# One more pair by block products, and sums of down weights moved: a SwiGLU, token mixer, SwiGLU layer on one core

## The chip, the core and the metric

The kernel runs on one core of a Trainium2 chip. The core has TensorE (PE in the profile, PEld for its weight loads), VectorE (DVE), ScalarE (ACT), GpSimd (POOL) and SyncE (SP), which here only issues DMAs. The metric is the device time of one launch in microseconds, the median of several runs. Before the change: 1127.27 us, median of 3 runs (1127.23 to 1127.75).

## What is computed

One decoder layer on x of 512 tokens by 1024, all in float32. The change touches its first part alone, a half-step SwiGLU block:

```python
def swiglu(x, w_gate, w_up, w_down):
    return (jax.nn.silu(x @ w_gate) * (x @ w_up)) @ w_down

h = rms_norm(x, ffn1_pre[l])
x = x + 0.5 * rms_norm(swiglu(h, ffn1_w_gate[l], ffn1_w_up[l], ffn1_w_down[l]), ffn1_post[l])
...
x = x + rms_norm(y, mix_post[l])
h = rms_norm(x, ffn2_pre[l])
x = x + 0.5 * rms_norm(swiglu(h, ffn2_w_gate[l], ffn2_w_up[l], ffn2_w_down[l]), ffn2_post[l])
```

The hidden width D_FF is 2816, 22 blocks of 128. The token mixer in the middle (y) stays as it is.

## The kernel before

**Precision.** Each float32 operand is split in two reduced parts: `split` (L110) casts the high part on ScalarE (L112) and subtracts it on VectorE (L119) for the low part. `mm3` (L139) then makes three matmuls of one: high by high, high by low, low by high. Names `whi` and `wlo` are the two parts of a weight tile, `xh_t` and `xl_t` those of the tokens.

**Gate and up.** The function `ffn` walks over 11 pairs of hidden blocks (256 columns of each weight). A pair has two forms.

- As single units (`classical`): four units, gate and up of each block, each 8 contraction tiles x 3 matmuls with all 512 tokens as 512 columns, 96 matmuls. Each unit needs its own 128x1024 piece of weights, split just before. The very first four units run as two halves of 256 tokens, since the tokens arrive in blocks of 128.
- By block products (`strassen`): gate and up of the pair are cut in blocks of contraction half and token half, and seven products of 24 matmuls with 256 columns replace the eight; 168 matmuls. The weights come as two tiles of the tag `raw` (three places), the first with the upper contraction half of gate (a11) and up (a21), the second with the lower half, up first (a22), then gate (a12). VectorE forms s1 = a21 + a22 (L377), a21 = a11 - a21 (L379), s2 = s1 - a11 (L383) and s2 = a12 - s2 (L388); each weight block is then split in high and low part. The products run in the order a11, a21, s2, a12, s1, a22, s2, and the second needs the difference a21. The other factor is sums of tokens in four kinds (`token_sums`, L507), made once per part.

The range `STRASSEN` (L48) says which pairs take the second form: in the first part pairs 3 to 10.

**Tokens' sums.** In the second part the blocks of tokens are kept whole when they are transposed (`full`, L226, copies from PSUM). In the first part they are not: `join` (L531) adds the high and low parts again, eight times, before the sums. The steps are handed out after single units by `STEPS` (L52), three each behind blocks 2 to 5.

**Sums of down weights.** The down projection of the part is also done by block products. It needs sums of the blocks of each pair's down weights. They are formed ahead, while gate and up run: the four blocks b11, b12, b21, b22 of a pair are loaded, `down_sums` (L481) overwrites them with four differences on VectorE (L484), and they are stored to a DRAM tensor `tdram` (L338, L494), to be read again by the down products. `weight_sums(p)` does this within pair p; pairs 10 and 9 are done ahead, in pairs 0 and 1 (`AHEAD`). `SUM_TAGS` names the buffers of each pair (KB, x, V, of: 128x512 each; other pairs use a `raw` tile).

**Down.** `ffn_down` (L579) runs seven products over the pairs: B11, T2, T3, T1, B21, B22, T4. For the last one, the first `EARLY` = 5 weights (T4 of pairs 0 to 4) are loaded during the product B21 into the place of `xl` and split before it begins.

**Order.** Each engine runs its list in order and waits on semaphores. The lists are made by a scheduler that reorders the program's instructions within their dependences; `issue_after` holds an instruction behind another. SP's list issues all large DMAs, in order; a DMA that waits for a buffer holds back those behind it. Buffers are places of a tag, taken in turn.

Of the kernel before, what the change touches and what calls it, by code (L numbers as in the profile page):

```python
# [12 lines left out]
F32 = mybir.dt.float32  # L13
# [14 lines left out]
NF = DFF // P  # L28
# [16 lines left out]
SPLIT_TAGS = dict(X=["Q"] * 4 + ["KA"] * 2, O=["V"] * 2 + ["KA"] * 2 + ["KB"] * 4 + ["SP"] * 11 + ["PT"] * 3,  # L45
                  Y=["PT"] * 5 + ["W"] * 2 + ["CB"] + ["Q"] * 4)
T_TAGS = ["NN"] * 3 + ["N"] + ["PT"] * 8 + ["CB"]
STRASSEN = range(3, NF // 2), range(1, NF // 2)  # L48
AHEAD = {0: 10, 1: 9}
SUM_TAGS = {2: ["KB"] * 4, 3: ["x"] * 4, 4: ["x"] * 4, 5: ["V"] * 4, 6: ["x"] * 4, 7: ["V"] * 4,  # L50
            8: ["of"] * 2 + ["V"] * 2}
STEPS = (0, 3, 3, 3, 3), (4, 2)  # L52
EARLY = 5
HOLD_TAGS = ["W"] * 2 + ["Q"] * 4 + ["KA"] * 2 + ["V"] * 2 + ["CB", "ring"]
PS_BUFS = dict(S=3, T=2, V=1, F=2)
# [4 lines left out]
OPEN = ("SS", "TT", "SS", "FF")  # L60
# [3 lines left out]
class Layer:  # L64
# [237 lines left out]
    def ffn(self, n, wg, wu, wd, post, finish, xsrc, tags, nps, aside=None):  # L302
# [5 lines left out]
        nc = self.nc  # L308
# [20 lines left out]
        def weight_sums(p):  # L329
            if n or p in AHEAD.values():  # L330
                return
            if p in SUM_TAGS:
                self.early_sums(p, wd, [self.slot(tag) for tag in SUM_TAGS[p]])
                return
            r = self.raw(wd[2 * p * P:(2 * p + 2) * P].rearrange("(e p) d -> p e d", p=P), [2, D])
            with self.tc.issue_after(self.last_rest):
                self.down_sums(*[r[:, e, h * S:(h + 1) * S] for e in range(2) for h in range(2)])
            nc.sync.dma_start(self.tdram[p], r.rearrange("p e (h d) -> p (e h) d", h=2))  # L338

        def block(src):  # L340
# [10 lines left out]
        def strassen(p):  # L351
# [95 lines left out]
        for p in range(NF // 2):  # L447
# [28 lines left out]
                self.split(hi, lo, ev)  # L476
            X.append(x)
            E.append((hi, lo))
        self.ffn_down(E, X, Y, wd, post, finish, xsrc)

    def down_sums(self, b11, b12, b21, b22):  # L481

        for out, x, y in ((b11, b12, b11), (b12, b22, b12), (b22, b22, b11), (b21, b21, b22)):
            self.nc.vector.tensor_sub(out, x, y)  # L484

    def early_sums(self, p, wd, places):

        blocks = [(i, h) for i in range(2) for h in range(2)]
        for (i, h), v in zip(blocks, places):
            self.nc.sync.dma_start(v, wd[(2 * p + i) * P:(2 * p + i + 1) * P, h * S:(h + 1) * S])  # L490
        with self.tc.issue_after(self.last_rest):
            self.down_sums(*places)
        for (i, h), v in zip(blocks, places):
            self.nc.sync.dma_start(self.tdram[p][:, 2 * i + h], v)  # L494

# [11 lines left out]
    def token_sums(self):  # L507


        nc = self.nc  # L510
        H = S // 2
        places = []
        for tag in T_TAGS:
            v = self.slot(tag, F32R, (P, D if tag == "NN" else S))
            places += [v[:, o:o + S] for o in range(0, v.shape[1], S)]
        kept, self.whole = self.whole, {}
        self.tsum = [([], []) for _ in range(4)]
        steps = []
        for c in range(2):
            hi, lo = [[v.rearrange("p (k c) -> p k c", k=2) for v in g]  # L520
                      for g in (places[8 * c:8 * c + 4], places[8 * c + 4:8 * c + 8])]
            if kept:
                whole = [kept[h][i][c] for i, h in ((0, 0), (1, 1), (0, 1), (1, 0))]
            else:
                whole = [self.slot("x").rearrange("p (k c) -> p k c", k=2) for _ in range(4)]
            f1, f2, f3, f4 = whole
            for i in range(4):
                for o, v in zip(self.tsum[i], (hi[i], lo[i])):
                    o.extend(v[:, k] for k in range(2))

            def join(dst, i, h, c=c):  # L531
                ks, cs = slice(4 * i + 2 * c, 4 * i + 2 * c + 2), slice(h * H, (h + 1) * H)
                nc.vector.tensor_add(dst, self.xht[:, ks, cs].bitcast(F32), self.xlt[:, ks, cs].bitcast(F32))

            def sub(dst, x, y):
                nc.vector.tensor_sub(dst, x, y)

            def parts(i, hi=hi, lo=lo, whole=whole):
                self.split(hi[i], lo[i], whole[i])

            def s1(f1=f1, f3=f3, join=join):
                join(f3, 0, 1)
                join(f1, 0, 0)
                sub(f1, f3, f1)

            def s2(f1=f1, f2=f2, f3=f3, join=join):
                join(f2, 1, 1)
                sub(f3, f2, f3)
                sub(f2, f2, f1)

            def s3(f2=f2, f4=f4, join=join):
                join(f4, 1, 0)
                sub(f4, f4, f2)

            def d1(f1=f1, f3=f3):
                sub(f1, f3, f1)

            def d2(f1=f1, f2=f2, parts=parts):
                sub(f2, f2, f1)
                parts(1)  # L560

            def d3(f2=f2, f3=f3, parts=parts):
                sub(f3, f2, f3)
                parts(2)

            def d4(f2=f2, f4=f4, parts=parts):
                sub(f4, f4, f2)
                parts(3)

            if kept:  # L570
                steps.append((d1, d3, d2, lambda p=parts: p(0), d4))
            else:
                steps += [s1, s2, lambda p=parts: p(0), s3, lambda p=parts: (p(1), p(2)), lambda p=parts: p(3)]
        if kept:
            a, b = steps
            return [a[0], a[1], b[0], b[1], a[2], b[2], a[3], b[3], a[4], b[4]]
        return steps

    def ffn_down(self, E, X, Y, wd, post, finish, xsrc):  # L579

        nc = self.nc
        NP = NF // 2
# [130 lines left out]
        def between():  # L713
            scaled(2, 0, c[0])
            r = self.rstd([ms[2, 0], ms[2, 1]], 2.0)
            while self.pending:
# [765 lines left out]
    def run(self, out):  # L1482
# [30 lines left out]
        with self.tc.manual_schedule(engines={ET.Activation, ET.DVE, ET.PE}):  # L1513
# [108 lines left out]
```

## Time and profile before

| | |
|---|---|
| median of 3 runs | 1127.27 us |
| the profiled execution, its own time | 1127.8 us |
| its span in the profile | 1125.6 us |
| mean granted clock of TensorE | 0.998 |
| gate and up of the first part, pairs 1 to 10 | from 37.1 to 242.0 us |
| pair 1, pair 2, pair 3 begin on TensorE | 37.1, 58.9, 80.6 us |

A page of the profile gives busy times of each engine over the whole span; views of the trace give the time line of one engine (start, duration, engine, line, operation, out<-in with partitions x elements; in brackets the idle time ahead and what ended it), the waits, and busy times by stretch. In the time line `SPq` rows are issues of DMAs, not their landings. The tile names are the program's with their numbers left out.

### The profile page before, as it was taken

How to read it: one execution, taken by the hardware profiler on the slowest of the kernel's cores; microseconds unless marked ns; L12 is line 12 of the kernel's file. 1: busy time of each engine (PE TensorE's matmuls, PEld its weight loads, DVE VectorE, ACT ScalarE, POOL GpSimd, SP SyncE). 2: the span in 40 equal slices, each digit the busy share in tenths (PEclk: the TensorE clock that was granted, in tenths of full speed). 3: DMA queues.
4: the chain of work that ended last, by engine and by line, in shares of the span. 5: the costliest groups of instructions: out<-in, count | busy, mean ns of one | idle time of the engine just before them, and what ended most of it. 6: DMA issues, size and time to landing. Idle time of an engine off the chain costs nothing.

```text
span 1125.6 us, 18656 instructions
## 1 busy us (share of the span) xinstructions
PE 1115.7 (99%) x6998; PEld 1004.2 (89%) x6998; DVE 911.2 (81%) x1565; ACT 646.8 (57%) x1169; POOL 79.2 (7%) x112
## 2 busy tenths in 40 slices
PE   9999999999999999999999999999999999999997
PEld 8889999998889987778888998888999999998886
DVE  7889999879677889687666688976898888979674
ACT  5435555567564778677565634645555555558562
POOL 1000000000012033243000000001000000000000
PEclk9999999999999999999999999999999999999999
DMA  9986665578863652211477758683323434356862
GB/s 318 331 283 224 185 208 173 153 267 293 265 206 108 196 132 85 68 37 47 147 246 237 243 174 289 203 290 121 101 87 126 129 112 126 100 187 228 290 224 82
DMA packets 153086, 206.04 MB, mean 183 GB/s; under 512 B 19842, under 2 KB 98210, under 8 KB 152740
## 3 DMA queue, kind: packets, MB, share of 16 engines
q1 hardware_dynamic: 152992, 204.85, 56.2%
q8 instruction: 55, 0.90, 0.3%
q14 instruction: 35, 0.29, 0.1%
q10 hardware_dynamic: 4, 0.00, 0.0%
HBM read 165.45 MB, written 39.37 MB: 182 GB/s over the span
## 4 chain that ended last, share of the span: by engine, by line
PE 90%; DVE 5%; ACT 2%; issue 1%; POOL 1%; DMA 1%; POOLq 0%; DVEq 0%; ACTq 0%
PE pb_F L141 11%; PE pb_F L143 11%; PE pb_F L142 11%; PE pb_S L143 8%; PE pb_S L142 8%; PE pb_S L141 8%; PE pb_T L143 6%; PE pb_T L142 6%; PE pb_T L141 6%; PE pb_V L143 3%; PE pb_V L142 3%; PE pb_V L141 3%; PE pb_V L1060 2%; PE pb_T L1045 1%; DVE SP_s L785 1%
## 5 line engine op out<-in xcount | busy, mean ns | idle before, releaser
L112 ACT CAST whi<-raw 128x1024 fp32r<-128x1024 f32 (+1 forms) x213 | 217.7, 1023 | 245.6 <-issue 71.1
L119 DVE TENSOR_TENSOR wlo<-raw,whi 128x1024 fp32r<-128x1024 f32 (+1 forms) x213 | 252.9, 1190 | 91.8 <-ACT whi L112 89.9
L141 PE MATMUL pb_F<-xh_t,whi 128*128 128x512 f32 (+1 forms) x392 | 142.0, 362 | 0.2 <-DVE Q_s L1270 0.2
L142 PE MATMUL pb_F<-xl_t,whi 128*128 128x512 f32 (+1 forms) x392 | 141.1, 360 | 0.0
L143 PE MATMUL pb_F<-xh_t,wlo 128*128 128x512 f32 (+1 forms) x392 | 141.0, 360 | 0.0
L112 ACT CAST whi<-tmp_t 128x1024 fp32r<-128x1024 f32 x55 | 57.6, 1048 | 57.4 <-PE pb_S L142 22.4
L119 DVE TENSOR_TENSOR wlo<-tmp_t,whi 128x1024 fp32r<-128x1024 f32 x55 | 67.3, 1224 | 23.2 <-ACT whi L112 21.8
L141 PEld LDWEIGHTS pb_F<-xh_t,whi 128*128 128x128 f32 x392 | 74.2, 189 | 9.9 <-DVE Q_s L1270 0.4
L143 PEld LDWEIGHTS pb_F<-xh_t,wlo 128*128 128x128 f32 x392 | 74.2, 189 | 9.6
L142 PEld LDWEIGHTS pb_F<-xl_t,whi 128*128 128x128 f32 x392 | 74.3, 190 | 9.3
L141 PE MATMUL pb_S<-xh_t,whi 128*128 128x256 f32 (+1 forms) x232 | 68.4, 295 | 0.0
L143 PE MATMUL pb_S<-xh_t,wlo 128*128 128x256 f32 (+1 forms) x232 | 68.3, 294 | 0.0
L142 PE MATMUL pb_S<-xl_t,whi 128*128 128x256 f32 (+1 forms) x232 | 68.3, 294 | 0.0
L1036 POOL TENSOR_SCALAR SP_s<-SP_s,st_t 128x384 f32<-128x384 f32 (+2 forms) x48 | 47.8, 1010 | 103.8 <-DVE st_t L972 76.3
L163 POOL TENSOR_TENSOR rs_t<-rs_t,mhalf_t 128x1 f32<-128x1 f32 x24 | 17.1, 711 | 538.1 <-DVE rs_t L159 538.0
L142 PE MATMUL pb_T<-xl_t,whi 128*128 128x256 f32 (+1 forms) x184 | 53.9, 293 | 0.0
L143 PE MATMUL pb_T<-xh_t,wlo 128*128 128x256 f32 (+1 forms) x184 | 53.8, 293 | 0.0
L141 PE MATMUL pb_T<-xh_t,whi 128*128 128x256 f32 (+1 forms) x184 | 53.7, 293 | 0.0
L141 PEld LDWEIGHTS pb_S<-xh_t,whi 128*128 128x128 f32 x232 | 44.5, 192 | 1.0
L142 PEld LDWEIGHTS pb_S<-xl_t,whi 128*128 128x128 f32 x232 | 44.5, 192 | 1.0
L143 PEld LDWEIGHTS pb_S<-xh_t,wlo 128*128 128x128 f32 x232 | 44.5, 192 | 0.9
L785 DVE CUSTOM_DVE_ANT_0 SP_s<-pb_S,W_s 128x128 f32<-128x128 f32 (+2 forms) x92 | 37.9, 441 | 7.0 <-PE pb_S L780 4.8
(839 smaller groups left out, 3425.3 us busy)
## 6 DMA issues: line engine op xcount, KB each, us to landing
raw<-in_ffn_w_up_dram SPq DMA_DIRECT2D x38, 512.0 KB, 4.9
raw<-in_ffn_w_gate_dram SPq DMA_DIRECT2D x37, 512.0 KB, 5.0
raw<-in_w_in_dram SPq DMA_DIRECT2D x18, 1024.0 KB, 5.5
raw<-in_ffn_w_down_dram SPq DMA_DIRECT2D x14, 1024.0 KB, 5.8
raw<-tdram SPq DMA_DIRECT2D x14, 1024.0 KB, 6.5
NN_s<-in_ffn_w_down_dram SPq DMA_DIRECT2D x22, 512.0 KB, 5.0
tdram<-NN_s SPq DMA_DIRECT2D x22, 512.0 KB, 4.4
odram<-ring_s SPq DMA_DIRECT2D x36, 128.0 KB, 3.2
```

Of the source, the lines that this page charges most:

```text
L112: self.last_cast = self.nc.scalar.copy(dsthi, src).ins
L119: self.last_rest = self.nc.vector.tensor_sub(dstlo, src, dsthi.bitcast(F32)).ins
L141: mm(out, lhi, rhi, start=start, stop=False, skip_group_check=skip)
L142: mm(out, lhi, rlo, start=False, stop=False, skip_group_check=skip)
L143: mm(out, llo, rhi, start=False, stop=stop, skip_group_check=skip)
L163: nc.gpsimd.tensor_tensor(out=r, in0=v, in1=self.mhalf, op=OP.pow)
L785: nc.vector.tensor_tensor_reduce(p, s, w, -1.0, FLOOR, OP.add, OP.min, st_m)
L1036: nc.gpsimd.tensor_scalar(pp, pp, st[:, 1, t:t + 1], None, op0=OP.mult)
L1045: nc.tensor.transpose(b[:, o + (t - kk) * P:o + (t - kk + 1) * P], pt[pn][:, po + kk * P:po + (kk + 1) * P], self.ident)
L1060: self.nc.tensor.matmul(out[:, kk * P:S], v, pp, start=first and kk == 0 and pi == 0, stop=False, skip_group_check=True)
```

## The change

The pair 2 of the first part takes block products instead of single units. The tokens' sums have to be ready one pair sooner: tokens 256 to 511 are now kept whole (eight copies on ScalarE), tokens 0 to 255 are still joined (four times instead of eight), and the steps are handed out as 5, 3 and 2 behind blocks 1 to 3, the last two inside pair 2. All sums of down weights from pair 2 on move one step later: those of pair p are made within pair p + 1. For the pairs 0, 1, 2, 9 and 10 the fourth difference (b21 - b22, after b22 has become b22 - b11) isn't formed there: b21 is stored as it is, and the last down product loads T2 and b21 of these five pairs and subtracts.

```diff
-STRASSEN = range(3, NF // 2), range(1, NF // 2)
+STRASSEN = range(2, NF // 2), range(1, NF // 2)
 AHEAD = {0: 10, 1: 9}
-SUM_TAGS = {2: ["KB"] * 4, 3: ["x"] * 4, 4: ["x"] * 4, 5: ["V"] * 4, 6: ["x"] * 4, 7: ["V"] * 4,
+DEFER = 0, 1, 2, 9, 10
+SUM_TAGS = {2: ["KB"] * 4, 3: ["x"] * 4, 4: ["V"] * 4, 5: ["x"] * 4, 6: ["V"] * 4, 7: ["of"] * 2 + ["V"] * 2,
             8: ["of"] * 2 + ["V"] * 2}
-STEPS = (0, 3, 3, 3, 3), (4, 2)
+STEPS = (5, 3, 2), (4, 2)
...
             rest_sums()
-            weight_sums(p)
+            if p - 1 in STRASSEN[n]:
+                weight_sums(p - 1)
...
-        for out, x, y in ((b11, b12, b11), (b12, b22, b12), (b22, b22, b11), (b21, b21, b22)):
+        for out, x, y in ((b11, b12, b11), (b12, b22, b12), (b22, b22, b11), (b21, b21, b22))[:3 + last]:
             self.nc.vector.tensor_sub(out, x, y)
...
-            def join(dst, i, h, c=c):
-                ks, cs = slice(4 * i + 2 * c, 4 * i + 2 * c + 2), slice(h * H, (h + 1) * H)
-                nc.vector.tensor_add(dst, self.xht[:, ks, cs].bitcast(F32), self.xlt[:, ks, cs].bitcast(F32))
+            def join(dst, i, c=c):
+                ks = slice(4 * i + 2 * c, 4 * i + 2 * c + 2)
+                nc.vector.tensor_add(dst, self.xht[:, ks, 0:H].bitcast(F32), self.xlt[:, ks, 0:H].bitcast(F32))
...
-        nc.sync.dma_start(xl[:, 0:EARLY].bitcast(F32), weights["T4"](0, EARLY))
+        if defer:
+            for k, o, m in ((0, 0, 3), (3, NP - 2, 2)):
+                for v, nm in ((xl, "T2"), (xh, "T4")):
+                    nc.sync.dma_start(v[:, k:k + m].bitcast(F32), weights[nm](o, m))
+        else:
+            nc.sync.dma_start(xl[:, 0:EARLY].bitcast(F32), weights["T4"](0, EARLY))
...
-            self.split(xh[:, ks], xl[:, ks], xl[:, ks].bitcast(F32))
+            src = xl[:, ks].bitcast(F32)
+            if defer:
+                d4 = self.sbt("tmp", [P, 2, S], bufs=2)[:, 0:ks.stop - k]
+                with self.tc.issue_after(self.last_rest):
+                    nc.vector.tensor_sub(d4, xh[:, ks].bitcast(F32), src)
+                src = d4
+            self.split(xh[:, ks], xl[:, ks], src)
...
-            t2 = self.norm_T(2, g, OPEN[2], sq2)
+            t2 = self.norm_T(2, g, OPEN[2], sq2, whole=True)
...
-            t3 = self.norm_T(3, g, OPEN[3], r=r3)
+            t3 = self.norm_T(3, g, OPEN[3], r=r3, whole=True)
```

The product of the down projection gets a first and a last index for this, since pairs 0, 1, 2, 9 and 10 come first in T4 and the walk then goes over pairs 3 to 8.

Two places show how the lists move. The first is SP's list in pair 1, where the weights of pair 2 are requested. Before: `raw_707` and `raw_738` are the gate and up weights of pair 2, `raw_604` is a tile of pair 1's down weights after its sums, `KB_s` are pair 9's down blocks.

```order
L490 DMA KB_s_681<-in_ffn1_w_down_dram 128x512
L475 DMA odram_73<-W_s_360 128x512
L490 DMA KB_s_682<-in_ffn1_w_down_dram 128x512
L95 DMA raw_707<-in_ffn1_w_gate_dram 128x8x256
L95 DMA raw_738<-in_ffn1_w_up_dram 128x8x256
L338 DMA tdram_72<-raw_604 128x2048
L494 DMA tdram_72<-KB_s_679 128x512
L494 DMA tdram_72<-KB_s_680 128x512
L494 DMA tdram_72<-KB_s_682 128x512
L494 DMA tdram_72<-KB_s_681 128x512
```

After, on SP at the same place: `raw_715` and `raw_718` are the two weight tiles of pair 2 in halves, `raw_622` is pair 1's tile of down sums, `KB_s_690` to `693` are pair 9's blocks, of which `692` is stored without a difference.

```order
L492 DMA KB_s_692<-in_ffn1_w_down_dram 128x512
L492 DMA KB_s_693<-in_ffn1_w_down_dram 128x512
L492 DMA x_s_1888<-in_ffn1_w_down_dram 128x512
L496 DMA tdram_72<-KB_s_692 128x512
L362 DMA raw_715<-in_ffn1_w_gate_dram 128x4x256
L362 DMA raw_715<-in_ffn1_w_up_dram 128x4x256
L339 DMA tdram_72<-raw_622 128x2048
L496 DMA tdram_72<-KB_s_690 128x512
L496 DMA tdram_72<-KB_s_691 128x512
L496 DMA tdram_72<-KB_s_693 128x512
L362 DMA raw_718<-in_ffn1_w_up_dram 128x4x256
L362 DMA raw_718<-in_ffn1_w_gate_dram 128x4x256
```

Pair 2's weights were two requests in a row ahead of pair 1's store; now the second tile stands behind that store and three more, and the first behind the store of pair 9's block as it came.

The second place is VectorE's list where TensorE goes from pair 1 to pair 2. Before, the last splits of pair 2's units and the tokens' steps stand here (`x_s` and `PT_s` are the tokens' sums, `KB_s_779` to `782` pair 2's down blocks):

```order
L484 TENSOR_TENSOR KB_s_779<-KB_s_780,KB_s_779 128x512
L467 TENSOR_TENSOR ring_s_530<-SP_s_695,ring_s_530 128x256
L484 TENSOR_TENSOR KB_s_780<-KB_s_782,KB_s_780 128x512
L468 TENSOR_TENSOR CP_s_506<-W_s_531,ring_s_530 128x256
L119 TENSOR_TENSOR Q_s_701<-ring_s_530,Q_s_700 128x512
L484 TENSOR_TENSOR KB_s_782<-KB_s_782,KB_s_779 128x512
L119 TENSOR_TENSOR wlo_796<-raw_707,whi_795 128x1024
L484 TENSOR_TENSOR KB_s_781<-KB_s_781,KB_s_782 128x512
L119 TENSOR_TENSOR wlo_825<-raw_738,whi_824 128x1024
```

After, on VectorE at the same place: the low part of a11, then s1 (`tmp_t_721`), the difference a21 (in `raw_715`), s2 (`tmp_t_722`), a product of pair 1 (`W_s_550`) and the low part of a21 (`wlo_758`):

```order
L120 TENSOR_TENSOR wlo_729<-raw_715,whi_728 128x1024
L378 TENSOR_TENSOR tmp_t_721<-raw_715,raw_718 128x1024
L380 TENSOR_TENSOR raw_715<-raw_715 128x1024
L384 TENSOR_TENSOR tmp_t_722<-tmp_t_721,raw_715 128x1024
L439 TENSOR_TENSOR W_s_550<-W_s_550,pb_S_661 128x512
L120 TENSOR_TENSOR wlo_758<-raw_715,whi_757 128x1024
L467 TENSOR_TENSOR SP_s_705<-ring_s_549,W_s_550 128x256
L120 TENSOR_TENSOR wlo_787<-tmp_t_722,whi_786 128x1024
```

What stood there waited for one weight tile at a time; now everything from `tmp_t_721` on stands behind the up half of the second tile.

More of the change, by code (lines that the diff above doesn't have):

```diff
@@ L336, in weight_sums @@
             with self.tc.issue_after(self.last_rest):
-                self.down_sums(*[r[:, e, h * S:(h + 1) * S] for e in range(2) for h in range(2)])
+                self.down_sums(*[r[:, e, h * S:(h + 1) * S] for e in range(2) for h in range(2)], p not in DEFER)
             nc.sync.dma_start(self.tdram[p], r.rearrange("p e (h d) -> p (e h) d", h=2))
@@ L478, in ffn, with down_sums @@
             E.append((hi, lo))
-        self.ffn_down(E, X, Y, wd, post, finish, xsrc)
-    def down_sums(self, b11, b12, b21, b22):
-        for out, x, y in ((b11, b12, b11), (b12, b22, b12), (b22, b22, b11), (b21, b21, b22)):
+        self.ffn_down(E, X, Y, wd, post, finish, xsrc, () if n else DEFER)
+    def down_sums(self, b11, b12, b21, b22, last=True):
+        for out, x, y in ((b11, b12, b11), (b12, b22, b12), (b22, b22, b11), (b21, b21, b22))[:3 + last]:
             self.nc.vector.tensor_sub(out, x, y)
@@ L491, in early_sums @@
         with self.tc.issue_after(self.last_rest):
-            self.down_sums(*places)
+            self.down_sums(*places, p not in DEFER)
         for (i, h), v in zip(blocks, places):
@@ L515, in token_sums @@
             places += [v[:, o:o + S] for o in range(0, v.shape[1], S)]
+        joined = 0 not in self.whole
+        if joined:
+            self.new_whole(0)
         kept, self.whole = self.whole, {}
@@ L521, in token_sums @@
                       for g in (places[8 * c:8 * c + 4], places[8 * c + 4:8 * c + 8])]
[L522 to L526, printed above, removed]
+            f1, f2, f3, f4 = whole = [kept[h][i][c] for i, h in ((0, 0), (1, 1), (0, 1), (1, 0))]
             for i in range(4):
@@ L539, in parts, with d1 @@
                 self.split(hi[i], lo[i], whole[i])
[L541 to L555, printed above, removed]
+            def d1(f1=f1, f3=f3, join=join):
+                if joined:
+                    join(f1, 0)
                 sub(f1, f3, f1)
@@ L568, in d4, with ffn_down @@
                 parts(3)
[L570 to L579, printed above, removed]
+            steps.append((d1, d3, d2, lambda p=parts: p(0), d4, lambda f4=f4, join=join: join(f4, 1)))
+        a, b = steps
+        return [a[0], a[1], b[0], b[1], a[2], b[2], a[3], b[3]] + ([a[5], b[5]] if joined else []) + [a[4], b[4]]
+    def ffn_down(self, E, X, Y, wd, post, finish, xsrc, defer):
         nc = self.nc
@@ L605, in split_next, with product @@
             parts[nm].append((hi, lo))
-        def product(a, wname, banks, start, stop, side=None, tail=0, keep=None, between=None, pre=()):
+        def product(a, wname, banks, start, stop, side=None, tail=0, keep=None, between=None, pre=(), begin=0, end=NP):
             held = []
@@ L613, in mm @@
                 hi, lo = a(k, t)
-                self.mm3(banks[t], hi, lo, w[0], w[1], start and k == 0, stop and k == NP - 1, True)
-            for k, w in enumerate(pre):
+                self.mm3(banks[t], hi, lo, w[0], w[1], start and k == 0, stop and k == end - 1, True)
+            for k, w in pre:
                 for t in range(2):
                     mm(t, k, w)
-            for k0 in range(len(pre), NP, 4):
-                n = min(4, NP - k0)
+            for k0 in range(begin, end, 4):
+                n = min(4, end - k0)
                 r = self.raw(weights[wname](k0, n), [n, S])
@@ L623, in product @@
                     m = min(2, n - k1)
-                    if keep and k0 + k1 + m > NP - tail:
+                    if keep and k0 + k1 + m > end - tail:
                         for j in range(m):
@@ L632, in product @@
                         k = k0 + k1 + j
-                        if k >= NP - tail:
+                        if k >= end - tail:
                             held.append((k, (hi[:, j], lo[:, j])))
@@ L720, in ffn_down @@
         product(half(parts["O"], 256), "T4", c, False, True, None, NP - EARLY, list(HOLD_TAGS), between,
-                [(xh[:, k], xl[:, k]) for k in range(EARLY)])
+                [(k, (xh[:, i], xl[:, i])) for i, k in enumerate(defer or range(EARLY))],
+                *((3, NP - 2) if defer else (EARLY, NP)))
         r = self.rstd([self.meansq(c[1], S, 2.0), ms[3, 1]], 2.0)
```

## The prediction

> **What bounds the kernel now.** I read the page first: TensorE is busy for the whole span. Then the list of who waited for whom, for TensorE alone.
>
> ```profile
> PE 1115.7 (99%) x6998; PEld 1004.2 (89%) x6998; DVE 911.2 (81%) x1565; ACT 646.8 (57%) x1169; POOL 79.2 (7%) x112
> PE pb_V L1511 <- POOL ident_t masks.py:199: 1.5, 1, 1.5
> PE pb_S L779 <- DVE SP_s L988: 0.2, 1, 0.2
> ```
>
> After the 1.5 us at the start no wait of TensorE is longer than 0.2 us, and none lies in the first part's gate and up. So the time is a sum of matmul slots. The change can gain only what it takes out of that sum; a wait that it adds counts in full. Freeing VectorE gains nothing by itself, since nobody on TensorE waits for it now.
>
> The stretches of the gate and up tell how near the next bound is. Columns: stretch, its length, then the busy time of TensorE, its weight loads, VectorE, ScalarE and GpSimd, the granted clock, the DMA share, GB/s.
>
> ```profile
> 0.00:37.20 37.20, 35.75 (x246) 32.62 (x247) 26.75 (x44) 20.84 (x37) 4.88 (x14) 1.00 1.00 334
> 12.00:37.20 25.20, 25.20 (x213) 25.15 (x212) 21.34 (x33) 13.83 (x23) 2.80 (x4) 1.00 1.08 369
> 37.20:58.85 21.65, 21.65 (x97) 17.91 (x96) 20.83 (x34) 6.95 (x10) 2.35 (x2) 1.00 0.90 304
> 59.00:80.77 21.77, 21.77 (x99) 18.04 (x98) 16.77 (x25) 6.73 (x10) 0.00 (x0) 1.00 0.89 286
> 100.92:121.07 20.15, 20.15 (x170) 20.15 (x170) 20.03 (x27) 10.92 (x15) 0.00 (x0) 1.00 0.67 215
> ```
>
> Pair 1 is the third row, pair 2 the fourth, pair 4 (by block products) the fifth. There VectorE is full too (20.03 of 20.15 us), and the DMA queue is close to full until pair 3 (0.89 to 1.08 of its 16 engines). Pair 2 is where VectorE had slack (16.77 of 21.77).
>
> **The change, part by part.** *Matmuls.* The time line of TensorE gives the slots; its columns are start, duration, then the instruction.
>
> ```profile
> 58.86 0.39 PE L141 MATMUL pb_S<-xh_t,whi 128*128 128x512 f32 x1
> 59.08 0.39 PE L142 MATMUL pb_S<-xl_t,whi 128*128 128x512 f32 x1
> 80.62 0.28 PE L141 MATMUL pb_S<-xh_t,whi 128*128 128x256 f32 x1
> 100.88 0.28 PE L141 MATMUL pb_T<-xh_t,whi 128*128 128x256 f32 x1
> 101.00 0.28 PE L142 MATMUL pb_T<-xl_t,whi 128*128 128x256 f32 x1
> 121.04 0.28 PE L141 MATMUL pb_S<-xh_t,whi 128*128 128x256 f32 x1
> ```
>
> Pair 2 runs from 58.86 to 80.62: 21.76 us for 96 matmuls of 512 columns (4 units x 8 x 3), 0.2267 each. Pair 4 runs from 100.88 to 121.04: 20.16 us for 168 of 256 columns (7 products x 8 x 3), 0.120 each. The change puts 168 of the second kind for 96 of the first: **-1.60 us**, and no other matmul changes. The Trainium skill, "TensorE: Matmul & The Clock Gate", section "Wait — 56ns, not 53.3ns?", puts the warm distance of matmuls at N / 2.4 GHz + 2.5 ns, so 215.8 and 109.2 ns here; by that the estimate is 20.72 - 18.34 = 2.4 us of gain. The rows show 226.7 and 120, so I take 1.60.
>
> *What pair 2 now needs earlier.* As single units, pair 2 needed one split weight after another. By block products the second product needs a21 = a11 - a21, formed behind s1 = a21 + a22, and a22 comes with the **second** weight tile. Before, this stood in front of pair 3:
>
> ```profile
> 75.22 1.23 DVE L377 TENSOR_TENSOR tmp_t<-raw 128x1024 f32<-128x1024 f32 x1 [2.16 <-DMA raw<-in_ffn_w_up_dram]
> 76.36 0.68 DVE L437 TENSOR_TENSOR ring_s<-ring_s,pb_T 128x512 f32<-128x512 f32 x1
> 79.03 1.22 DVE L379 TENSOR_TENSOR raw<-raw 128x1024 f32<-128x1024 f32 x1
> 80.16 1.22 DVE L383 TENSOR_TENSOR tmp_t<-tmp_t,raw 128x1024 f32<-128x1024 f32 x1
> 81.44 1.23 DVE L119 TENSOR_TENSOR wlo<-raw,whi 128x1024 fp32r<-128x1024 f32 x1
> 82.59 0.68 DVE L437 TENSOR_TENSOR W_s<-W_s,pb_V 128x512 f32<-128x512 f32 x1
> ```
>
> VectorE idled 2.16 us for the load and began s1 at 75.22; the low part of a21 was ready at 81.44 + 1.23 = 82.67, and TensorE wanted it at 80.62 + 24 x 0.120 + 0.24 = 83.74. A margin of 1.07 us, behind a load. In the changed order s1, a21, s2, a product of 128x512 and the low part stand directly behind each other: 3 x 1.14 + 0.60 + 1.22 = 5.24 us from s1's start S (steps of 1.14 and 0.60 from these rows' starts), 5.29 with 0.05 to be noticed. TensorE reaches pair 2 at 58.86 as before and wants that low part at 58.86 + 2.88 + 0.24 = 61.98. So TensorE **waits S - 56.7 us**, and everything turns on when the second tile's up half (a22) lands.
>
> *When it lands.* Up to and with that load the changed SP order holds 18.74 MB (tiles counted from the code). Three readings. (a) If the queue never idles: 334 GB/s x 37.2 us = 12.4 MB by 37.2, the other 6.3 MB at 369 GB/s take 17.1 us: S = 54.3, no wait. (b) Before, 18.74 MB end with the last of four stores to tdram from KB:
>
> ```profile
> L494 SPq DMA_DIRECT2D tdram<-KB_s x1: 320/320/320, 55.3 to 55.3; - x1
> DMA to landing us min/median/max: 4.2/4.2/4.2
> ```
>
> issued at 55.3, landed 4.2 later: S = 59.5, a wait of 2.8. (c) By its chain of waits:
>
> ```profile
> 29.66 0.35 SPq L338 DMA_DIRECT2D tdram<-raw  x1
> ...
> 46.94 0.38 SPq L95 DMA_DIRECT2D raw<-in_ffn_w_up_dram  x1
> 47.54 0.40 SPq L338 DMA_DIRECT2D tdram<-raw  x1
> L338 SPq DMA_DIRECT2D tdram<-raw x1: 402/402/402, 47.5 to 47.5; - x1
> DMA to landing us min/median/max: 8.7/8.7/8.7
> tdram<-KB_s SPq DMA_DIRECT2D x12, 256.0 KB, 4.8
> KB_s<-in_ffn_w_down_dram SPq DMA_DIRECT2D x12, 256.0 KB, 5.7
> raw<-in_ffn_w_up_dram SPq DMA_DIRECT2D x38, 512.0 KB, 4.9
> tdram<-raw SPq DMA_DIRECT2D x2, 1024.0 KB, 8.6
> ```
>
> On SP the loads for pair 2 now stand behind the store of pair 9's unsummed block, which waits for that block's load, which waits for a KB place that a store of pair 10's sums has to leave. Those stores follow the reload of the third raw place, whose old content must have been stored first; that store lands at about 38.2 now (29.66 issue and 8.6), so they go out near 38.4. Then 4.8 (store) and 5.7 (load) give 48.9 for pair 2's first issue. Its first tile and a store of 1 MB are 2.10 MB, the same as the two rows at 46.94 and 47.54, which took 47.54 + 8.7 - 46.94 = 9.3 us: 58.2. Three KB stores and the a22 half, 1.31 MB at 304 to 369 GB/s, take 3.6 to 4.3: S = 62.1, a wait of 5.4. I take the middle of (b) and (c), **S = 60.8 and a wait of 4.1 us**, because both are this queue's own rows, while (a) needs a queue that the rows show idling (0.90 from 37.2 on). The ends stay: 0 to 5.4.
>
> The Trainium skill, "DMA: Bandwidth & Descriptors", section "Anatomy of one DMA — SWDGE (gpsimd) path", fits a DMA as 2.0 us + bytes / 436 GB/s. By it chain (c) is 38.4 + 2.6 + 2.6 + 2.0 + 7.8 = 53.4 (an estimate), and the wait is gone. It is fitted for GpSimd's path, and the row of 512 KB here has 4.9 us where it gives 3.2; so I count it to the first rival.
>
> *VectorE's work.* Pair 2 gets seven low parts for four (3 x 1.14), four sums of 1.14 and two of 0.60: 9.2 us more. Out go the fourth down sums of five pairs and four sums of tokens (9 x 0.60 = 5.4), and one step of delay moves four sums per pair behind. In pair 2: 16.77 - 4 x 0.60 (its down sums go to pair 3) + 9.2 = 23.6, less some five steps of 0.60 on the tokens that now stand ahead of it = 20.6, against 20.16 of TensorE. That is 0.4 over, and VectorE's idle time in front of S, or the wait itself, hides it: nothing, or 0.4 us if that cover is gone. ScalarE gets eight copies of 128x256 between 21 and 25 us:
>
> ```profile
> 29.70 1.05 ACT L112 CAST whi<-raw 128x1024 fp32r<-128x1024 f32 x1 [6.17 <-DMA raw<-in_ffn_w_gate_dram]
> ```
>
> There it idled 6.17 us for a load; nothing.
>
> *The last down product.* Three more subtractions (2.9 us) and 1.31 MB more of loads:
>
> ```profile
> 285.00:315.00 30.00, 30.00 (x134) 24.85 (x133) 20.61 (x24) 16.09 (x19) 0.00 (x0) 1.00 0.78 258
> ```
>
> VectorE has 9.4 us free in these 30, and the sums are wanted only after the product before. Nothing; up to 1 us if the next weight tile, queued behind the added loads, comes late.
>
> *Sum.* -1.6 + 4.1 = **+2.5 us**. The profiled execution took 1127.8 us (span 1125.6 and 2.2 around it), 0.5 over the median of 1127.27; I add to the median: **1129.8**. What a measurement here can tell from no change is about 0.2%, 2.25 us.
>
> **The rivals.** *The load comes in time* (for: reading (a), since the loads before it are issued earlier than they were; against: (b), (c), and the same sum that waited 2.16 us for a load before pair 3). The wait is 0 to 2.8 us, the net -1.6 to +1.2: 1125.7 to 1128.5. This is the other side, not slower; it decides at S = 59.5 and is pure gain from S = 56.7. *The load comes later still*: pauses of the queue as long as the 2.16 us above, or the late weight tile of the down products; net +3.8 to +5.3, up to 1132.6. Against: the queue ahead is full and needs no start. *The wider gain*: 2.4 us by the skill's slot and no wait, 1124.9; the rows of 0.120 speak against it. That the change doesn't do what it says can be ruled out by the order: 72 more matmul rows, as 168 - 96.
>
> **How the numbers follow.** The forecast, a wait of 2.8 to 5.4 us, 1128.5 to 1131.1: 0.58. In time: 0.25. Later: 0.14. Wider gain: 0.03. The bound of 2.25 over cuts the forecast at a wait of 3.9, 0.36 of it above. So slower by over 0.2%: 0.36 + 0.14 = 0.50; within: 0.22 + 0.25 = 0.47; faster: 0.03. The range takes in the pure gain, 1125.7, and the late load, 1132.6; the likeliest case alone has 1128.5 to 1131.1.
>
> **What would show it.** Pair 2 should hold 168 matmuls, and outside one gap last 20.16 us. The gap should stand 24 matmuls into pair 2, with "whi" of ScalarE and then "wlo" of VectorE as releaser; VectorE's s1 should show idle time of several us in front of it, ended by the load of the up weights. If that row starts before 56.7 I am wrong on the queue; if TensorE waits in pair 3 or later, on VectorE; if near 315 to 325, on the last down product.

## The result, and the profile after

The changed kernel takes 1137.30 us, the median of 4 runs (1136.96 to 1138.64), against 1127.51 before (the median of four runs; 1127.27 was that of the first three): a ratio of 1.0085, 95% interval 1.0073 to 1.0097. That is 9.8 us slower, where +2.5 was forecast and 1132.6 was the end of the range. The side was right, the size was not. The profiled execution took 1136.97 us and spans 1134.9, 9.3 more than the span before.

First the busy times on the page of the changed kernel, then from its list of TensorE's waits the three longest besides the 1.5 us at the start, which the kernel before has too (line waited for, us in total, times, longest):

```profile
PE 1117.7 (98%) x7070; PEld 1007.9 (89%) x7070; DVE 916.9 (81%) x1569; ACT 654.4 (58%) x1185; POOL 75.8 (7%) x112
PE pb_V L142 <- ACT whi L113: 5.9, 1, 5.9
PE pb_V L144 <- DVE wlo L120: 0.9, 1, 0.9
PE pb_F L218 <- DVE tmp_t L213: 0.8, 1, 0.8
```

TensorE's time line (start, duration) shows where the two long ones stand:

```profile
61.84 0.28 PE L144 MATMUL pb_T<-xh_t,wlo 128*128 128x256 f32 x1
68.01 0.58 PE L142 MATMUL pb_V<-NN_s,whi 128*128 128x256 f32 x1 [5.89 <-ACT whi L113]
68.39 0.41 PE L143 MATMUL pb_V<-N_s,whi 128*128 128x256 f32 x1
69.74 0.58 PE L144 MATMUL pb_V<-NN_s,wlo 128*128 128x256 f32 x1 [0.94 <-DVE wlo L120]
...
74.30 0.28 PE L142 MATMUL pb_S<-NN_s,whi 128*128 128x256 f32 x1
```

The gap stands after 24 matmuls of pair 2, at its second product, and behind it the matmuls are slow: the 22 from 69.74 to 74.30 take 4.56 us, where 22 x 0.120 = 2.64 is their time at the usual step. That is 1.9 us more. The windows name the reason in the column of the granted clock (third from the end):

```profile
62.00:64.00 2.00, 0.12 (x1) 0.00 (x0) 0.00 (x0) 0.00 (x0) 0.00 (x0) 1.00 1.09 358
66.00:68.00 2.00, 0.00 (x0) 0.00 (x0) 2.00 (x3) 1.04 (x1) 0.00 (x0) 0.76 1.08 357
70.00:72.00 2.00, 2.00 (x10) 2.00 (x11) 2.00 (x4) 1.02 (x3) 0.00 (x0) 0.50 0.45 106
74.00:76.00 2.00, 2.00 (x19) 2.00 (x19) 2.00 (x4) 1.57 (x3) 0.00 (x0) 1.00 0.98 354
```

VectorE's time line shows what the gap waits for. The first row is s1, the fifth the low part of a21:

```profile
64.34 1.22 DVE L378 TENSOR_TENSOR tmp_t<-raw 128x1024 f32<-128x1024 f32 x1 [5.80 <-DMA raw<-in_ffn_w_up_dram]
65.60 1.23 DVE L380 TENSOR_TENSOR raw<-raw 128x1024 f32<-128x1024 f32 x1
66.74 1.22 DVE L384 TENSOR_TENSOR tmp_t<-tmp_t,raw 128x1024 f32<-128x1024 f32 x1
67.88 0.68 DVE L439 TENSOR_TENSOR W_s<-W_s,pb_S 128x512 f32<-128x512 f32 x1
68.47 1.22 DVE L120 TENSOR_TENSOR wlo<-raw,whi 128x1024 fp32r<-128x1024 f32 x1
```

That low part is ready at 69.69. Pair 2 began at 59.09, 0.23 later than before, so it was wanted at 62.2: it is 7.5 us late.

The rest shows at the end of the part: a matmul inside the down products, then the first transposes after the last of these products. The changed kernel, then the kernel before:

```profile
315.42 0.39 PE L142 MATMUL pb_F<-whi,SP_s 128*128 128x512 f32 x1
...
351.22 1.03 PE L218 MATMUL pb_S<-ident_t,tmp_t 128*128 128x128 f32 x8
353.02 1.32 PE L218 MATMUL pb_F<-ident_t,tmp_t 128*128 128x128 f32 x8 [0.77 <-DVE tmp_t L213]
354.09 0.47 PE L142 MATMUL pb_T<-W_s,KB_s 128*128 128x512 f32 x1
```

```profile
307.55 0.39 PE L141 MATMUL pb_F<-whi,SP_s 128*128 128x512 f32 x1
...
342.69 1.03 PE L217 MATMUL pb_S<-ident_t,tmp_t 128*128 128x128 f32 x8
343.56 1.04 PE L217 MATMUL pb_F<-ident_t,tmp_t 128*128 128x128 f32 x8
344.35 0.48 PE L141 MATMUL pb_T<-W_s,SP_s 128*128 128x512 f32 x1
```

Call the difference of two such starts the lag. The first matmul on `SP_s` in the down products stood at 307.55 and now stands at 315.42, a lag of 7.9. It is 351.22 - 342.69 = 8.5 at the first transposes and 354.09 - 344.35 = 9.7 behind the second. So the end of the part costs 1.9. The sum behind pair 2 is 0.2 (its later start) - 1.6 (matmuls) + 7.5 (wait) + 1.9 (clock) = 8.0, of which 7.9 is left in the down products; with 1.9 at the end it is 9.7 (the parts are rounded). Of this 0.4 is made up in the later parts (the span is 9.3 longer).

### The profile page after: what moved, and what is told of

Its sections match the earlier page's. It is cut to its first block, busy times and chain, and to the rows that moved or that the text cites. A ratio compares the mean times of both kernels' runs of the same rounds, so it can differ in the third digit from the quotient of the medians.

```text
span 1134.9 us, 18836 instructions
## 1 busy us (share of the span) xinstructions
PE 1117.7 (98%) x7070; PEld 1007.9 (89%) x7070; DVE 916.9 (81%) x1569; ACT 654.4 (58%) x1185; POOL 75.8 (7%) x112
## 4 chain that ended last, share of the span: by engine, by line
PE 85%; DVE 6%; DMA 3%; ACT 2%; issue 1%; SPq 1%; POOL 1%; POOLq 0%; DVEq 0%; ACTq 0%
PE pb_F L142 11%; PE pb_F L144 11%; PE pb_F L143 11%; PE pb_S L144 7%; PE pb_S L143 7%; PE pb_S L142 7%; PE pb_T L144 5%; PE pb_T L143 5%; PE pb_T L142 5%; PE pb_V L144 2%; PE pb_V L143 2%; PE pb_V L142 2%; PE pb_V L1056 2%; PE pb_T L1041 1%; DMA KB_s<-in_ffn_w_down_dram 1%
## 5 line engine op out<-in xcount | busy, mean ns | idle before, releaser
L113 ACT CAST whi<-tmp_t 128x1024 fp32r<-128x1024 f32 x58 | 60.8, 1049 | 61.4 <-PE pb_S L143 23.4
L120 DVE TENSOR_TENSOR wlo<-tmp_t,whi 128x1024 fp32r<-128x1024 f32 x58 | 70.8, 1221 | 23.2 <-ACT whi L113 21.9
L143 PE MATMUL pb_T<-xl_t,whi 128*128 128x256 f32 x184 | 52.0, 283 | 0.0
L144 PE MATMUL pb_T<-xh_t,wlo 128*128 128x256 f32 x184 | 52.0, 283 | 0.0
L142 PE MATMUL pb_T<-xh_t,whi 128*128 128x256 f32 x184 | 52.0, 283 | 0.0
L120 DVE TENSOR_TENSOR PT_s<-pb_T,PT_s 128x512 fp32r<-128x512 f32 (+1 forms) x72 | 39.3, 560 | 5.6 <-ACT PT_s L113 4.6
```

What stands on the lines that cost most here:

```text
L113: self.last_cast = self.nc.scalar.copy(dsthi, src).ins
L120: self.last_rest = self.nc.vector.tensor_sub(dstlo, src, dsthi.bitcast(F32)).ins
L142: mm(out, lhi, rhi, start=start, stop=False, skip_group_check=skip)
L143: mm(out, lhi, rlo, start=False, stop=False, skip_group_check=skip)
L144: mm(out, llo, rhi, start=False, stop=stop, skip_group_check=skip)
```

## The experiments

S is the start of the first sum that reads the second tile's up half (in the order a21 first, that is s2). Times are medians, the ratio is against the kernel before on the same chip.

| run | edit to the changed kernel | S, us | us | ratio, 95% interval |
|---|---|---|---|---|
| the change | | 64.3 | 1137.30 | 1.0073 to 1.0097 |
| e1 | pair 2 as single units | | 1135.08 | 1.0050 to 1.0080 |
| e3 | a21 first | 67.0 | 1137.95 | 1.0069 to 1.0103 |
| e6, e7 | 48, 72 unread matmuls in the gap | 66.8, 65.3 | 1138.78, 1135.73 | 1.0074 to 1.0114, one run |
| e8 | pair 1's sums in pair 10 | 57.0 | 1130.23 | 1.0015 to 1.0034 |
| g3 | steps 0, 5, 3 | 58.1 | 1131.18 | 1.0019 to 1.0043 |
| g8 | g3 and e8 | 53.2 | 1129.77 | 1.0014 to 1.0033 |
| g9 | g8 and e3 | 53.9 | 1132.08 | 1.0025 to 1.0055 |
| h1 | g8, sums of pairs 2 and 9 on GpSimd | 55.0 | 1130.82 | 1.0021 to 1.0048 |
| h4 | g3, sums in their own pair | 57.4 | 1133.44 | 1.0034 to 1.0059 |
| h2 | g8, no deferral | 49.1 | 1125.82 | 0.9973 to 0.9990 |
| h3 | h1, no deferral | 53.5 | 1130.91 | 1.0018 to 1.0041 |
| i1 | no deferral, nothing else | 55.9 | 1125.96 | 0.9978 to 0.9996 |
| i2 | steps 0, 5, 3, no deferral | 51.8 | 1126.23 | 0.9981 to 0.9999 |
| i3 | h2 with pair 2 as single units | | 1127.10 | 0.9989 to 1.0007 |
| j2 | b21 copied onto itself | 55.5 | 1128.10 | 0.9994 to 1.0012 |

### Is it the block products? (e1, e3)

```diff
-STRASSEN = range(2, NF // 2), range(1, NF // 2)
+STRASSEN = range(3, NF // 2), range(1, NF // 2)
```

> Theory A (late tile): the cost sits at the second product of pair 2, which waits for the second weight tile; with pair 2 as single units again nothing waits there and the matmuls are those of before, so what stays is the end of the part (some 0.7 us in the last down product, 1.0 us at the transposes behind it): 1129.3 us, between 1128.5 and 1130.5, no wait of TensorE over 1 us between 55 and 85 us. Rival B (moved work): the sums moved one step later and the deferred differences cost most of it wherever pair 2 stands: 1134 to 1137 us.

Measured 1135.08: theory A failed in its simple form, and rival B's time came true. The longest wait of this run, and a window behind it:

```profile
PE pb_S L142 <- ACT whi L113: 2.7, 1, 2.7
62.00:64.00 2.00, 1.96 (x4) 1.14 (x5) 1.10 (x1) 0.34 (x1) 0.00 (x0) 0.50 1.06 386
```

Even as single units pair 2 waits, here for its **first** tile, at 58 to 62 us, and the clock halves behind the gap. ScalarE had idled 15.9 us ahead of that unit's cast, for the load of the gate weights. So the loads of pair 2 are late as such, whatever reads them.

```diff
-            nc.vector.tensor_add(s1, a21, a22)
             w = block(a11)
...
-            nc.vector.tensor_sub(s2, s1, a11)
+            nc.vector.tensor_sub(s2, a22, a21)
+            nc.vector.tensor_add(s1, s2, a11)
```

> The differences are formed in another order (a21 = a11 - a21 from the first tile alone, then s2 = a22 - a21, then s1 = s2 + a11; the same sums, rounded in another order), SP's list of loads is the same to the second tile. Theory A: the tile lands at 64.3 us as in the changed kernel; now only the third product needs it, whose low part is ready at 64.3 + 1.14 + 1.04 + 1.22 = 67.8 and is wanted at 65.1: a wait of 2.7 us in place of 7.5, and no slow matmuls behind it if a short gap leaves the clock alone: 1137.3 - 9.4 + 2.7 = 1130.6 us, between 1129.8 and 1131.8. Rival B (VectorE has too much to do in pair 2, the load is not what is late): the wait is as long as before, 1136 to 1138 us. If the clock falls behind a short gap too: 1132 to 1133.

Measured 1137.95, as slow as the change. The tile landed still later in this run (S = 67.0), the wait moved to the third product as told (5.0 us, behind a copy that ScalarE does after the late cast), and the clock halved again. A shorter dependence does not help against a load that comes that late. Theory B's time came true, but its reason (VectorE) did not: VectorE idled in front of S here as well.

### The clock (e6, e7)

```diff
             product(r11, w, b11, True, False)
+            if (n, p) == (0, 2):
+                for _ in range(2):
+                    product(r7, w, b11, True, True)
             w = block(a21)
```

> 48 matmuls that nobody reads stand between the first and the second product of pair 2 (5.76 us, in a bank that the second product starts anew), so TensorE works through most of the gap of 5.9 us. Theory C (the idle gap closes the clock): the granted clock stays 1.00, the 24 matmuls behind the gap take 0.12 us each in place of 0.213, and 1.9 us are gained: 1135.4 us, between 1134.8 and 1136.0. Rival (the slow matmuls have another cause, such as weight loads or memory): they stay slow, 1137 to 1138 us.

No answer: with S at 66.8 the 48 matmuls ended 3.3 us too early, a gap stayed and the clock fell to 0.50 behind it. With three products (72):

> 72 matmuls that nobody reads between the first and the second product of pair 2 (8.64 us), since 48 ended before a later tile in their run. Theory C: with idle time under 1.5 us the granted clock stays 1.00 from 56 to 82 us, and the 24 matmuls behind take 0.12 us each. Rival: they take 0.213 all the same.

From 56 to 82 us the clock stayed 1.00. In e7's time line the second product begins with steps of 0.12:

```profile
70.55 0.28 PE L144 MATMUL pb_V<-xh_t,wlo 128*128 128x256 f32 x1
70.67 0.28 PE L142 MATMUL pb_V<-NN_s,whi 128*128 128x256 f32 x1
70.79 0.28 PE L143 MATMUL pb_V<-N_s,whi 128*128 128x256 f32 x1
```

So it is the idle gap that halves the clock, and the 1.9 us are its price: a term of the change's sum. The Trainium skill, "TensorE: Matmul & The Clock Gate", section "Part 1: The HAM clock gate", has half rate after at least one idle window of about 3.4 us. The trace agrees on the half rate; on the length it does not: gaps of 2.7 us (e1) and 1.8 us (h1) had 0.50 behind them too, while after 1.6 us (e8) and 1.9 us (g9) the clock stayed 1.00. So the length of a gap alone doesn't decide it.

### What stands ahead in the queue (e8, g3, g8, g9)

```diff
-                weight_sums(p - 1)
+                weight_sums(p - 1 if p < NF // 2 - 1 else 1)
...
-                weight_sums(p)
+                if (n, p) != (0, 1):
+                    weight_sums(p)
```

> The sums of pair 1's down weights are made in pair 10 in place of pair 1: a load and a store of 1 MB and three subtractions go out of the queue ahead of pair 2's weights, and a place of the weight tiles is free for the first of them. Theory A: the first tile is requested near 39 us, the second near 51 us with nothing large ahead of it, lands near 55.5, before 56.7: no wait, no slow clock, 1137.3 - 9.4 = 1127.9 us, between 1127.0 and 1129.2. Rival B (VectorE's work in pair 2): a wait of 4 us or more stays, 1132 us or more.

S went from 64.3 to 57.0, and 7.1 of the 9.8 us with it; waits of 1.6, 0.8 and 0.4 us stayed. So theory A holds on the load, short of the whole. In the change's own lists I then saw five steps on the tokens ahead of pair 10's sums on VectorE, whose stores free KB's places for pair 9's blocks, behind which pair 2's weights stand. I took that for the cause (theory D):

```diff
-STEPS = (5, 3, 2), (4, 2)
+STEPS = (0, 5, 3), (4, 2)
```

> The tokens' steps are handed out as 0, 5 and 3 behind blocks 1 to 3 in place of 5, 3 and 2; nothing else differs. Theory D (VectorE's list makes the tile late): the five steps stood ahead of pair 10's sums on VectorE, so KB's places came free 10 us later and pair 9's blocks and pair 2's weights followed; without them the stores from KB go out near 28 to 33 us, pair 2's first tile is requested by 48 and its second lands before 56.7: no gap over 1 us in pair 2, 1137.3 - 9.4 = 1127.9 us, between 1127.0 and 1129.5. Rival E (the bytes in the queue decide, whoever waits for whom): the second tile still lands after 60, 1132 us or more.

1131.18, S = 58.1: 6.1 us better than the change, but 3.3 short of what was told, and S is still behind 56.7. Theory D is part of it at most.

> The steps as 0, 5, 3 and pair 1's sums in pair 10. Theory D: the second tile stands ahead of the stores and lands some 5 us earlier than it is wanted; what is left over the time before is the end of the part (0.8 us in the last down product): 1127.5 - 1.6 + 0.8 = 1126.7 us, between 1126.2 and 1128.0. Rival E: as long as with pair 1's sums late alone, 1130.2.

1129.77: not told apart from e8 alone, although S is 53.2, well ahead of the 56.7 that is needed. Here VectorE idled 4.3 us in front of S and then was busy for 25.8 of the 26 us from 56 to 82; in pair 2 TensorE waited 0.4 and 0.7 us for it, and 0.8 us for a copy of ScalarE that stood behind a cast waiting for VectorE.

> As the one before, and a21 from the first tile alone (the same sums in another order). Theory D: the second tile is in time already, so the order of the differences changes nothing: within 0.7 us of the one before. Rival (VectorE's order at the start of pair 2 still holds TensorE, as with pair 1's sums late, where the low part of the first product stood behind the first sum): 1 to 2 us faster than the one before.

1132.08: not faster than g8; whether the 2.3 us over it are real is not shown, since there are four runs and the intervals of the two overlap. In the profiled execution, the fastest of the four at 1130.13, the other order of the three differences has one wait of 1.9 us at the third product and the 0.7 us of g8, and mends nothing.

### Is VectorE too full? (h1, h3, h4)

```diff
+        if p in (9, 2):
+            self.down_sums(*places, p not in DEFER, self.nc.gpsimd)
+        else:
...
```

> Steps as 0, 5, 3, pair 1's sums in pair 10 (1129.77 us without more), and the down sums of pairs 9 and 2 on GpSimd in place of VectorE. Theory F (with the loads in time VectorE's work is what holds TensorE in pair 2: it is busy 25.8 of 26 us there, and TensorE waits 0.8, 0.7 and 0.4 us): 1.8 us of sums leave VectorE in pair 2, 1.2 us or so are gained: 1128.5 us, between 1127.5 and 1129.3. Rival G (GpSimd's subtractions slow VectorE's, or hold KB's places longer than VectorE did): 1129.8 or more.

> The two before together. If both theories hold, their gains add: 1127.6 us, between 1126.6 and 1128.6, for the first time level with the kernel before or under it. Rivals: 1129.8 or more.

Both came out by rival G, 1130.82 and 1130.91. GpSimd's rows in h1, and VectorE's behind them:

```profile
39.96 2.75 POOL L487 TENSOR_TENSOR KB_s<-KB_s 128x512 f32<-128x512 f32 x1 [19.95 <-DMA KB_s<-in_ffn_w_down_dram]
43.46 2.66 POOL L487 TENSOR_TENSOR KB_s<-KB_s 128x512 f32<-128x512 f32 x2 [0.74 <-DMA KB_s<-in_ffn_w_down_dram]
46.66 0.45 DVE L793 CAST dm_t<-SP_s 128x512 f32<-128x512 int32 x1 [5.10 <-POOL SP_s L791]
```

The first subtraction took 2.75 us (0.68 on VectorE), and a small index fill that GpSimd owes VectorE stood behind it and two more: VectorE idled 5.1 us, and TensorE waited 1.8 in pair 1. A queue with nothing in it is free only if nobody waits for what comes next.

```diff
-            if p - 1 in STRASSEN[n]:
-                weight_sums(p - 1)
+            weight_sums(p)
```

> Steps as 0, 5, 3 (1131.18 us without more), and the sums of down weights from pair 2 on made in their own pair again. Theory F: VectorE gets three subtractions more in pair 2, where it is full, and later pairs have what they had: 1131.2 + 1.8 = 1133.0 us, between 1132.0 and 1134.5, with longer waits of TensorE in pair 2 or 3. Rival (the step's delay is worth nothing, VectorE has room): 1131.2, within 0.7.

1133.44 (the buffers' tags are those of before): as theory F said, 2.3 more than g3, though the intervals of the two overlap. Its wait of 1.5 us at pair 2's first product is no evidence for F: that low part stands behind S, and VectorE forms pair 2's sums only from 78.68 on. Behind them stands a wait of 0.75 us in pair 3 that g3 doesn't have. So that the sums are better made one step later where pair 2 is full is likely, and not shown for sure.

### Without the deferral (h2, i1, i2, i3)

```diff
-DEFER = 0, 1, 2, 9, 10
+DEFER = ()
```

> Steps as 0, 5, 3, pair 1's sums in pair 10 (1129.77 us without more), and no pair deferred: all four differences are formed ahead, the last down product loads one tensor as before. Theory: the last down product and the transposes behind it give back 1.3 us (the difference of the starts against the kernel before grows from 0.70 at 305 us to 1.96 at 345), and three more subtractions of 0.60 in pairs 1 to 3 cost up to 1: 1129.0 us, between 1128.2 and 1129.8, with the growth between 305 and 345 us under 0.4. Rival (the growth has nothing to do with the deferral): it stays over 1 us, 1129.8 to 1131.

1125.82, faster than the kernel before and 4.0 under g8, where 0.8 was expected. VectorE has five sums more in gate and up, and TensorE no longer waits there: VectorE's list from S on is that of g8 with the fourth sum in it, but it begins at S = 49.1, behind 1.26 us of idle time and not 4.3. Which of the three edits matters?

> The changed kernel with no pair deferred, and nothing else changed: the tokens' steps still stand ahead of pair 10's sums. Theory D (the steps alone make the second tile late): it still lands after 60, 1135 us or more, only the end of the part gives 1 to 2 us back. Theory H (the deferral is the larger part: without it the second tile is requested ahead of the store of 1 MB and three more in SP's list, 1.8 MB or 5 us of queue at 350 GB/s): it lands near 58 to 59, the wait is 1 to 2 us and the clock stays: 1129.0 us, between 1127.5 and 1131.

> Steps as 0, 5, 3 and no pair deferred, pair 1's sums left in pair 1: two numbers of the change undone, the rest kept. If the two causes add: the second tile is in time, no wait, 1127.5 - 1.6 = 1125.9 us, between 1125.4 and 1127.0, level with the version that also moves pair 1's sums (1125.82). If moving pair 1's 2 MB is needed too: 1127.5 to 1130, with a wait of 1 us or more in pair 2.

The deferral alone: i1 takes 1125.96, ratio 0.9987 (0.9978 to 0.9996), and i2 is level with it. Theory D fell with i1, where the five steps stand ahead as in the change, and S is 55.9, in time. H's reason stands, and its price was too small. SyncE's list shows how. The changed kernel, then i1 (start, how long the issue took or, for several, their stretch):

```profile
15.12 0.90 SPq L492 DMA_DIRECT2D of_s<-in_ffn_w_down_dram  x2
21.44 0.33 SPq L496 DMA_DIRECT2D tdram<-KB_s  x1
22.90 0.41 SPq L96 DMA_DIRECT2D raw<-in_ffn_w_gate_dram  x1
...
46.00 1.62 SPq L492 DMA_DIRECT2D KB_s<-in_ffn_w_down_dram  x3
47.71 0.38 SPq L492 DMA_DIRECT2D x_s<-in_ffn_w_down_dram  x1
50.36 0.33 SPq L496 DMA_DIRECT2D tdram<-KB_s  x1
50.77 0.39 SPq L362 DMA_DIRECT2D raw<-in_ffn_w_gate_dram  x1
51.85 0.58 SPq L339 DMA_DIRECT2D tdram<-raw  x1
52.53 2.71 SPq L496 DMA_DIRECT2D tdram<-KB_s  x3
55.33 1.26 SPq L362 DMA_DIRECT2D raw<-in_ffn_w_up_dram  x1
```

```profile
15.05 0.91 SPq L492 DMA_DIRECT2D of_s<-in_ffn_w_down_dram  x2
16.86 0.38 SPq L898 DMA_DIRECT2D w_t<-in_nsa_w_ck_dram  x1
20.14 0.37 SPq L96 DMA_DIRECT2D raw<-in_ffn_w_gate_dram  x1
...
39.85 5.75 SPq L492 DMA_DIRECT2D KB_s<-in_ffn_w_down_dram  x4
46.79 0.38 SPq L362 DMA_DIRECT2D raw<-in_ffn_w_gate_dram  x1
47.22 1.63 SPq L362 DMA_DIRECT2D raw<-in_ffn_w_up_dram  x2
50.89 0.34 SPq L339 DMA_DIRECT2D tdram<-raw  x1
52.09 6.01 SPq L496 DMA_DIRECT2D tdram<-KB_s  x4
```

With the deferral, b21 needs no sum, so its store stands right behind its load, and SyncE can do nothing else until that load has landed: from 16.0 to 21.4 for pair 10's block (pair 1's weights go out 2.8 us later, at 22.90 and not 20.14) and from 48.1 to 50.4 for pair 9's. And the up half of pair 2's second tile, which in i1 is the second of the two issues in the row at 47.22, ahead of the store of 1 MB, is requested at 55.33, behind it and three more. Both come with the early store; which of them counts for more, no run separates.

> The version at 1125.82 us (steps 0, 5, 3, pair 1's sums in pair 10, no deferral) with pair 2 as single units again. If its gain is the matmuls of pair 2, -1.60 us, and nothing else: 1127.4 us, between 1126.9 and 1128.0. If the gain comes from the other edits: 1125.8, within 0.5.

1127.10 against 1125.82 with block products: pair 2's own worth is 1.3 us, somewhat under the 1.60 forecast, and the other edits of h2 gain nothing by themselves.

### The deferral with its store put back (j2)

```diff
             self.nc.vector.tensor_sub(out, x, y)
+        if not last:
+            self.nc.vector.tensor_copy(b21, b21)
```

> The changed kernel, deferral and all, with one copy of b21 onto itself on VectorE in the place of the subtraction that was left out: VectorE has as much to do as without deferral, and b21's store again waits for VectorE. SP's list is then that of the version without deferral: no store right behind its own load, and pair 2's second tile ahead of the stores. Theory M (the early store and the order of SP's list are the loss in pair 2; the loads and subtractions at the last down product are the rest): pair 2 loses nothing, the end of the part keeps 1 to 2 us: 1126.0 + 1.3 = 1127.3 us, between 1126.5 and 1128.5, though work is added. Rival (the deferral loses its time in another way, at the end of the part or on VectorE): 1135 us or more.

1128.10, 9.2 under the change though five copies are added. Where pair 2's weights are requested, SyncE's list is i1's again (the up half of the second tile at 49.16, the store of 1 MB behind it at 49.76), S = 55.5, and pair 2 loses nothing. What is left is the end of the part:

```profile
306.99 0.39 PE L142 MATMUL pb_F<-whi,SP_s 128*128 128x512 f32 x1
...
344.94 1.31 PE L218 MATMUL pb_F<-ident_t,tmp_t 128*128 128x128 f32 x8 [1.09 <-DVE tmp_t L213]
346.01 0.47 PE L142 MATMUL pb_T<-W_s,KB_s 128*128 128x512 f32 x1
```

The lag is 306.99 - 307.55 = -0.6 in the down products and 346.01 - 344.35 = +1.7 behind the transposes: 2.2 us. In i1 the same rows have no gap:

```profile
306.36 0.39 PE L142 MATMUL pb_F<-whi,SP_s 128*128 128x512 f32 x1
...
341.50 1.03 PE L218 MATMUL pb_S<-ident_t,tmp_t 128*128 128x128 f32 x8
342.37 1.04 PE L218 MATMUL pb_F<-ident_t,tmp_t 128*128 128x128 f32 x8
343.16 0.48 PE L142 MATMUL pb_T<-W_s,SP_s 128*128 128x512 f32 x1
```

There the lag is -1.2 at all three places (306.36 - 307.55, 341.50 - 342.69 and 343.16 - 344.35). The other traces say the same: between the first place and the last the lag grows in all twelve kernels with the deferral, by 1.0 (e8) to 2.4 us (g3), and in none of the five without it. In each of the twelve 0.6 to 0.7 us of this lies ahead of the transposes. So the deferral has two prices, and both are shown: the place of b21's store in SyncE's list, and 1 to 2.4 us at the end of the part. What at the end costs them, the added loads, the subtractions or the other order of the pairs, is open.

## Why the prediction was wrong

- **The matmuls, -1.60: nearly right.** i3 against h2 measures -1.3.
- **Where TensorE waits: right.** The gap stands 24 matmuls into pair 2, released by "whi" and then "wlo", and s1 has 5.80 us of idle time ended by the load of the up weights. The rule, a wait of S - 56.7, gives 64.34 - 56.7 = 7.6 where 7.5 was measured, and the versions with S under 56.7 and no backlog on VectorE (i1, i2, h2, j2) do not wait in pair 2.
- **When the tile lands: this is the step that failed.** It took S = 60.8, the middle of readings (b) and (c), and S is 64.3. Reading (c), the chain of waits, was the right one and too early at its start. It had the KB stores out at 38.4 and 4.8 us until they land; three stores go out one after another from 39.40 to 41.3, so the next loads start at 46.0 and not at 43.2; these land 1.3 us sooner than thought, and pair 2's first issue is at 50.77 and not 48.9. From there its legs fit: 50.77 + 9.3 + 4.3 = 64.4. That makes 2.2 of the 3.5 us by which S was early; the other 1.3 went by taking the middle with (b), which was a row of another list: the stores that (b) counts to were no longer where they had been.
- **The clock: left out.** The sum charged a wait of 4.1 us at its length. Idle time of that size has half the clock behind it: 1.9 us in the change, shown by e7.
- **VectorE's work, nothing to 0.4: right for the change, where the wait covers it, and too low without that cover.** g8, with the load in time but VectorE idle until 53.2, waits 1.9 us in pair 2; idle time ahead of S is not a reserve when VectorE is full from S on.
- **The last down product, "nothing; up to 1 us": too low.** It is 1.9 us in the change and 2.2 in j2, most of it at the transposes behind the product, which was not looked at.
- **The rivals.** "The load comes later still" is what happened, at nearly twice its price (up to +5.3 against +9.8), since neither the clock nor the end of the part was in it. The forecast also took the deferral for a saving of VectorE's time with a small price at the end. That its stores, with no sum ahead of them, would hold SyncE was in the change's own list (the rows of pair 9's b21 were shown there), and was counted as one wait on the chain, not as what put the chain there.

In sum, by this trace: the wait was 3.4 us longer than the 4.1 charged, and 1.9 of clock and 1.9 at the end were not charged at all. These are 7.2 of the 7.3 us between +2.5 and +9.8.

The one-line version i1 (1125.96 us) and h2 (1125.82) are faster than the kernel before by 0.04 to 0.27% by their intervals: block products in pair 2 and the moved sums together were good for about 1.4 us (1127.32 - 1125.96 in i1), and the deferral cost 11.3 (1137.30 - 1125.96).

## What to carry to other kernels

Taking a sum away from in front of a store makes the store ready as soon as its load has landed; if one queue issues both in order, look where the store now stands, because all loads behind it wait for that landing. In these runs every wait of TensorE of 2.2 us or more in gate and up had slow matmuls behind it; such a wait is to be charged with them, not by its length alone. When two readings of one landing time disagree, take the one that walks through the new list, and walk each store on its own.

## What the runs showed of the hardware that was not expected

- Half the granted clock followed gaps as short as 1.8 us (h1), and in the change it lasted from the restart at 68.0 to 73.9 us. It did not follow 1.6 us (e8), nor 1.9 us (g9), a longer gap than h1's. In h1 it came about 1 us after the restart at 50.48: the matmuls there stand 0.23 us apart up to 51.28 and 0.42 from 51.55. What decides between such gaps, the runs don't tell.
- The same list of loads lands at different times: with one SyncE list up to the second tile, S was 64.3 in the change, 66.8 in e6 and 65.3 in e7, and e6's four runs spread from 1134.87 to 1140.14 us, where those of i1, i2, i3, h2 and j2, which have no such wait, stay within 1.9 each.
- A subtraction of 128x512 on GpSimd took 1.3 to 2.75 us (six in h1, median 1.46), against 0.68 on VectorE.
